# One Newton chain for the input norm's four tiles, mixer weights and last-tile statistics on VectorE, and the transposed memory reloaded in layer 1

## The chip, the cores and the metric

The kernel runs on one core of a Trainium2 chip. The metric is the device time of one execution in microseconds (us). Engines are named as in the profile: TensorE is PE (its weight loads PEld), VectorE is DVE, ScalarE is ACT, GpSimd is POOL, SyncE is SP, which here only issues transfers.

## The reference

A trunk of two layers over x (512 tokens, 1024 features), in float32, behind an input layer norm. Each layer has three parts, and each part ends in `h = layer_norm(alpha * h + part)`:

```
h = layer_norm(x, ln0_g, ln0_b)
for l in range(2):
    mix = hybrid_mixer(h, ...)            # u = silu(layer_norm(conv31(c_a * sigmoid(c_g)))),
                                          # o = rms_norm(gated linear attention(q, k, v, a)) * silu(r)
                                          # mix = concat([u, o]) @ w_mix_out
    h = layer_norm(alpha * h + mix, ln1)
    xa = memory_cross_attention(h, mem, w_xq, w_xkv, w_xo)   # K, V = split(mem @ w_xkv), 256 memory tokens, 4 heads
    h = layer_norm(alpha * h + xa, ln2)
    h = layer_norm(alpha * h + swiglu(h, w_ffn_in, w_ffn_out), ln3)
```

The mixer's causal depthwise convolution is 31 wide over 512 channels, its linear attention goes in chunks of 64 tokens with 4 heads.

## The kernel before, in words

The 512 tokens are four tiles of 128 (h[0] to h[3]). Every matrix product is done in three passes (`mm3`, L148 to L150): each operand is split into a high part, a rounded copy that ACT writes (L102), and a low part, the difference to it, that VectorE or POOL writes (L103); the products are high times high, low weight times high, and high weight times low. A weight chunk of 128x1024 is loaded by SP into one of four `raw` tiles (`wchunk`, L134), and its low part goes to the next engine of a list set by `wlo_engines` (L107).

Names in the rows: `mem` is the 256 memory tokens, `mT` its transpose (high and low, 1 MB each), made by TensorE's transposes into `mt` (`mem_T`, L621) and read by the key and value products of the cross-attention, `pp_xk` into `KT` and `pt_xv` into `V`. `w_c`, `w_qk`, `w_v`, `w_r` are chunks of the mixer's input weights, `w_xk`, `w_xv` of the memory's, `w_mo` of the mixer's output weights; `pp_c` is the convolution's input product. `cvt` and `cvb` are the transposes before and behind the convolution's own norm (`v_cln`, `y_cln`, `b`; `acc` is ACT's normalized result, L883), `csl` its silu, `cUh` and `cUl` the high and low parts of the result; `po`, `ms`, `y_rms`, `og`, `ogt`, `cOh` belong to the attention group's rms norm. `po_mo`, `po_xo`, `po_fo` are the three parts' output products.

The input norm (L665 to L677) works tile by tile: statistics (`bn_stats`, `bn_aggr`), then 1/sqrt by an integer guess and Newton steps (`rstd_of`, from L152: eleven VectorE instructions per tile with those around it), then b, then one ACT activation that scales h. `layer_norm` (L192) does the other norms: the sums of a tile come from the accumulating VectorE instruction that adds a product to h (L298), the squares from an ACT pass over the whole tile (L200), then two VectorE scalings by the mean (L206), the Newton steps, two scalings by the result (L211), and the transposes for the next product (`lt_ln`, L219, into `hT_ln`) or, behind the last norm, the store (L213).

In layer 1, `mem_T` loads the memory again (SP, L617) and transposes it again, among the mixer's input products. `aside` is a list of transfers that are issued one by one right behind weight loads (`behind`). A scheduler sets the order of the instructions on each engine from the order in the code, priorities and the buffers of its pools.

## Time and profile before

| | us |
|---|---|
| median of 3 runs | 1413.37 (1412.58, 1413.37, 1416.64) |
| profiled execution | 1412.22 |
| its span | 1410.5 |
| PE busy | 1379.3 (98%) |
| DVE busy | 1071.8 (76%) |
| ACT busy | 682.2 (48%) |
| POOL busy | 183.1 (13%) |

The span is the time between the first and the last instruction in the trace; the profiled execution's own time has 1.72 us around it. Busy time is the sum over an engine's instructions without those that only issue transfers. Times in timelines are counted from the start of the span.

### The profile page before, as it was taken

What the parts mean: (1) busy time and instruction counts of PE and PEld (TensorE: products, weight loads), DVE (VectorE), ACT (ScalarE), POOL (GpSimd) and SP (SyncE); (2) the same over time, 40 slices, a digit from 0 to 9 for tenths busy, and PEclk for the clock granted to TensorE, in tenths of its full rate; (3) what the DMA queues carried; (4) which work ended last, traced back from release to release, by engine and by line L of the source; (5) the groups of instructions that cost most, each with busy time, mean ns of one, the idle gap of its engine ahead of it and who ended that gap; (6) DMA issues with size and microseconds to landing.
All of it is one profiled execution on the core that took longest, in us unless ns stands there. A gap on an engine that the chain in (4) does not pass through costs nothing.

```text
span 1410.5 us, 22543 instructions
## 1 busy us (share of the span) xinstructions
PE 1379.3 (98%) x8847; PEld 1235.4 (88%) x8847; DVE 1071.8 (76%) x1911; ACT 682.2 (48%) x1122; POOL 183.1 (13%) x130
## 2 busy tenths in 40 slices
...
GB/s 256 154 90 91 90 168 146 256 237 134 76 153 147 220 164 138 180 181 126 101 141 89 90 91 164 239 151 257 204 61 123 176 141 197 171 135 203 156 135 60
DMA packets 131198, 214.80 MB, mean 152 GB/s; under 512 B 8956, under 2 KB 83408, under 8 KB 131092
## 3 DMA queue, kind: packets, MB, share of 16 engines
...
q10 hardware_dynamic: 288, 0.26, 0.1%
...
## 4 chain that ended last, share of the span: by engine, by line
PE 88%; DVE 4%; ACT 3%; DMA 3%; issue 1%; SPq 0%; DVEq 0%; ACTq 0%; POOLq 0%
PE fx L551 5%; PE fx L553 5%; PE fx L552 5%; PE fw L551 3%; PE fw L553 3%; PE fw L552 3%; PE pp_xq L149 2%; PE pp_xq L148 2%; PE pp_c L148 2%; PE pp_c L149 2%; PE pp_xq L150 2%; PE pp_c L150 2%; PE po_xo L148 2%; PE po_xo L149 2%; PE po_xo L150 2%; PE po_mo L148 2%
## 5 line engine op out<-in xcount | busy, mean ns | idle before, releaser
L750 DVE SCALAR_TENSOR_TENSOR cv<-u,chan,cv 128x511 f32<-128x511 f32 (+29 forms) x240 | 159.9, 729 | 0.2
L103 DVE TENSOR_TENSOR w_s<-s,w_s 128x1024 fp32r<-128x1024 f32 x80 | 97.7, 1221 | 38.3 <-ACT w_s L102 38.3
L102 ACT ACTIVATE w_s<-s 128x1024 fp32r<-128x1024 f32 x80 | 84.6, 1057 | 66.2 <-DMA s<-raw_a 42.1
L306 POOL DMA_DIRECT2D s<-raw_a x40 | 34.7, 880 | 628.6 <-DVE h L495 186.9
L551 PE MATMUL fx<-T_ln,w_s 128*128 128x256 f32 x320 | 90.7, 284 | 0.4 <-ACT u L564 0.2
L552 PE MATMUL fx<-T_ln,w_s 128*128 128x256 f32 x320 | 90.5, 283 | 0.0
L553 PE MATMUL fx<-T_ln,w_s 128*128 128x256 f32 x320 | 90.4, 283 | 0.0
L200 ACT ACTIVATE junk<-h,nm_ln 128x1024 uint8<-128x1024 f32 x24 | 27.6, 1150 | 113.2 <-DVE nm_ln L198 110.8
L102 ACT ACTIVATE w_a<-raw_a 128x1024 fp32r<-128x1024 f32 x60 | 63.1, 1057 | 30.6 <-PE foX_fo L514 13.0
L103 DVE TENSOR_TENSOR w_a<-raw_a,w_a 128x1024 fp32r<-128x1024 f32 x60 | 73.2, 1220 | 4.4 <-ACT w_a L102 4.1
L551 PEld LDWEIGHTS fx<-T_ln,w_s 128*128 128x128 f32 x320 | 61.4, 192 | 0.9 <-ACT u L564 0.8
L552 PEld LDWEIGHTS fx<-T_ln,w_s 128*128 128x128 f32 x320 | 61.4, 192 | 0.0
L553 PEld LDWEIGHTS fx<-T_ln,w_s 128*128 128x128 f32 x320 | 61.4, 192 | 0.0
L149 PE MATMUL pp_xq<-hT_ln,w_xq 128*128 128x256 f32 (+1 forms) x192 | 61.3, 322 | 0.0
L148 PE MATMUL pp_xq<-hT_ln,w_xq 128*128 128x256 f32 (+1 forms) x192 | 60.3, 321 | 0.5 <-ACT hT_ln L102 0.5
L150 PE MATMUL pp_xq<-hT_ln,w_xq 128*128 128x256 f32 (+1 forms) x192 | 60.1, 318 | 0.0
L149 PE MATMUL pp_c<-hT_ln,w_c 128*128 128x512 f32 (+1 forms) x160 | 56.6, 356 | 0.0
L148 PE MATMUL pp_c<-hT_ln,w_c 128*128 128x512 f32 (+1 forms) x160 | 55.4, 360 | 0.6 <-DVE h L298 0.4
L150 PE MATMUL pp_c<-hT_ln,w_c 128*128 128x512 f32 (+1 forms) x160 | 55.9, 351 | 0.0
L102 ACT ACTIVATE w_S_fo<-raw_S_fo 128x1024 fp32r<-128x1024 f32 x32 | 33.9, 1060 | 36.0 <-PE foX_fo L514 14.2
L149 PE MATMUL po_xo<-w_xo,oTh 128*128 128x512 f32 x128 | 49.9, 392 | 0.0
L306 POOL DMA_DIRECT2D S_fs<-w_ffn_out x16 | 17.2, 1073 | 249.1 <-DMA S_fs<-w_ffn_out 187.1
...
## 6 DMA issues: line engine op xcount, KB each, us to landing
raw_a<-w_ffn_in SPq DMA_DIRECT2D x60, 512.0 KB, 4.7
s<-raw_a POOLq DMA_DIRECT2D x40, 512.0 KB, 5.3
raw_fo<-w_ffn_out SPq DMA_DIRECT2D x36, 512.0 KB, 4.3
S_fs<-w_ffn_out SPq DMA_DIRECT2D x32, 512.0 KB, 5.3
raw_S_fo<-S_fs SPq DMA_DIRECT2D x32, 512.0 KB, 3.7
s<-w_ffn_in SPq DMA_DIRECT2D x20, 512.0 KB, 3.5
raw_xv<-w_xkv SPq DMA_DIRECT2D x16, 512.0 KB, 5.7
raw_c<-w_in SPq DMA_DIRECT2D x16, 512.0 KB, 5.0
```

Source lines behind the costliest of these rows:

```text
L102: ACT.activation(hi, src, AF.Copy)
L103: eng.tensor_sub(lo, src, f(hi))
L148: PE.matmul(o, lh, rh, start=start, stop=False)
L149: PE.matmul(o, lh, rl, start=False, stop=False)
L150: PE.matmul(o, ll, rh, start=False, stop=stop)
L200: ACT.activation(junk, ht, AF.Square, bias=nm, accum_out=v)
L306: POOL.dma_start(dst, src, accum_op=ALU.add, max_dma_last_dim=4096)
L551: PE.matmul(o, wh, bh, start=start and k == 0, stop=False, skip_group_check=True)
L552: PE.matmul(o, wh, bl, start=False, stop=False, skip_group_check=True)
L553: PE.matmul(o, wl, bh, start=False, stop=stop and k == 3, skip_group_check=True)
L750: DVE.scalar_tensor_tensor(cv[ct][:, s:], u[:, ct, :T - s], wj, cv[ct][:, s:], ALU.mult, ALU.add)
```

## The change

It has five parts.

1. The input norm collects the statistics of the four tiles in one table and runs one chain of Newton steps on 128x4 elements; all four ACT activations come behind it. In front of it, the low parts of the second half of `w_xv` are all made by VectorE, where VectorE and POOL took turns.
2. The low parts of layer 0's `w_mo` are all made by VectorE, where VectorE and POOL took turns (layer 1 had VectorE before).
3. In each of the six norms behind a product, the last token tile takes its mean and variance from VectorE's `bn_stats` and `bn_aggr`, without the accumulating sums and ACT's square. In the last norm of all the statistics go by 256 columns, in the others by 512.
4. Layer 0 writes the transposed memory, high and low, to DRAM (two SP transfers of 1 MB, behind the first two loads of `raw_xk`). Layer 1 reads them back with two transfers that POOL issues, and has no loads, transposes and splits of the memory.
5. Two tables that are used once move from a pool of their own to a shared one.

The diff, without the lines that only move a name:

```diff
@@ -81,7 +81,7 @@
     ident = const.tile([P, P], F32, name="ident")
     make_identity(nc, ident)
     causal = const.tile([P, CH], U8, name="causal")
-    causal_f = const.tile([P, CH], F32, name="causal_f")
+    causal_f = tmp.tile([P, T], F32, tag="t", name="causal_f")[:, :CH]
 
     POOL.memset(causal_f, 1.0)
     for i in range(2):
@@ -191,15 +191,19 @@
 
     def layer_norm(tt, sums, gb, name, hT=None, store=None):
 
+
         ht = h[tt]
         nm = small.tile([P, 1], F32, tag="nm", name=f"nm_{name}{tt}")
-        for x in sums[2:]:
-            DVE.tensor_scalar(sums[0], sums[0], x, None, ALU.add)
-        DVE.tensor_scalar(nm, sums[0], sums[1], -1.0 / D, ALU.add, ALU.mult)
         v = small.tile([P, 1], F32, tag="v", name=f"v_{name}{tt}")
-        ACT.activation(junk, ht, AF.Square,
-                       bias=nm, accum_out=v)
-        DVE.tensor_scalar(v, v, VS / D, VS * EPS, ALU.mult, ALU.add)
+        if isinstance(sums, list):
+            DVE.tensor_scalar(nm, sums[0], sums[1], -1.0 / D, ALU.add, ALU.mult)
+            ACT.activation(junk, ht, AF.Square, bias=nm, accum_out=v)
+            DVE.tensor_scalar(v, v, VS / D, VS * EPS, ALU.mult, ALU.add)
+        else:
+            mv = small.tile([P, 2], F32, tag="mv", name=f"mv_{name}{tt}")
+            DVE.bn_aggr(mv, sums)
+            DVE.tensor_scalar(v, mv[:, 1:2], EPS, VS, ALU.add, ALU.mult)
+            DVE.tensor_scalar(nm, mv[:, 0:1], -1.0, None, ALU.mult)
         tail = store is not None and tt == NT - 1
         for i in range(2):
             s = slice(i * 512, (i + 1) * 512)
@@ -293,12 +297,18 @@
                 cs = slice(*cols[c])
                 mm3(bks[c][:, :cols[c][1] - cols[c][0]], stat[k][0][:, tsl], stat[k][1][:, tsl],
                     wh[:, 0, cs], wl[:, 0, cs], k == 0, k == nk - 1)
-            st = small.tile([P, 3], F32, tag="sums", name=f"sums_{name}{tt}") if norm is not None else None
+            sw = 256 if last and fin else 512
+            if norm is not None:
+                st = ln_stats(tt, name, D // sw) if last else \
+                    small.tile([P, 2], F32, tag="sums", name=f"sums_{name}{tt}")
             for c, (c0, c1) in enumerate(cols):
-                DVE.scalar_tensor_tensor(h[tt][:, c0:c1], h[tt][:, c0:c1], scale, bks[c][:, :c1 - c0],
-                                         ALU.mult, ALU.add, accum_out=st[:, c:c + 1] if norm is not None else None)
+                DVE.scalar_tensor_tensor(h[tt][:, c0:c1], h[tt][:, c0:c1], scale, bks[c][:, :c1 - c0], ALU.mult, ALU.add,
+                                         accum_out=st[:, c:c + 1] if norm is not None and not last else None)
+                if norm is not None and last:
+                    for x0 in range(c0, c1, sw):
+                        DVE.bn_stats(st[:, x0 // sw, :], h[tt][:, x0:x0 + sw])
             if norm is not None:
-                norm(tt, [st[:, c:c + 1] for c in range(len(cols))])
+                norm(tt, st if last else [st[:, c:c + 1] for c in range(2)])
 
 
     def add_into(dst, src):
@@ -606,6 +616,18 @@
             dest.first(j, sg, uu)
 
 
+    mdram = [dram.tile([P, NK, MEM], F32, tag=f"mT{j}", name=f"mT{j}_dram") for j in range(2)]
+
+    def mem_views(mT):
+        return lambda kt: (mT[0][:, kt, :], mT[1][:, kt, :])
+
+    def mem_again(l):
+
+        mT = [block([P, NK, MEM], F32R, f"mT{j}_{l}") for j in range(2)]
+        for j in range(2):
+            POOL.dma_start(mT[j], mdram[j])
+        return mem_views(mT)
+
     def mem_T(name):
 
         mT = [block([P, NK, MEM], F32R, f"mT{j}_{name}") for j in range(2)]
@@ -622,7 +644,7 @@
                 ks, ms_ = slice(i * 4, i * 4 + 4), slice(mt * P, (mt + 1) * P)
                 split(mT[0][:, ks, ms_], mT[1][:, ks, ms_], pt.rearrange("p (k t) -> p k t", k=4))
 
-        return lambda kt: (mT[0][:, kt, :], mT[1][:, kt, :]), part
+        return mT, part
 
     def new_K(l):
         return [block([P, NK, MEM], F32R, f"KT{j}_{l}") for j in range(2)]
@@ -645,16 +667,16 @@
         for tt in tts:
             nc.sync.dma_start(h[tt], a["x"][0, tt * P:(tt + 1) * P, :])
 
-    mT, mem_part = mem_T("0")
+    mT_tiles, mem_part = mem_T("0")
+    mT = mem_views(mT_tiles)
     mem_part((0, 0))
-    lnrow = const.tile([2 * NK, P], F32, name="lnrow")
+    lnrow = tmp.tile([P, T], F32, tag="t", name="lnrow")[:2 * NK, :P]
     V = new_V(0)
     wlo_engines(DVE)
     mem_V(0, mT, V, 0, first=lambda: mem_part((1, 0), (0, 1), (1, 1)))
     load_x(0, 1, 2, 3)
     nc.sync.dma_start(lnrow[0:NK, :], a["ln0_g"].rearrange("(k p) -> k p", p=P))
     nc.sync.dma_start(lnrow[NK:2 * NK, :], a["ln0_b"].rearrange("(k p) -> k p", p=P))
-    wlo_engines(DVE, POOL)
     mem_V(0, mT, V, 1)
     pl = bank("lncol_ps", tag="tr")
     PE.transpose(pl[:, :2 * NK], lnrow, ident[:2 * NK, :2 * NK])
@@ -663,18 +685,19 @@
     KT = new_K(0)
     hT = new_hT("ln0")
     with tc.high_priority(offset=HP):
+        mv0 = const.tile([P, NT, 2], F32, name="mv0")
+        v0 = const.tile([P, NT], F32, name="v0")
+        b0 = const.tile([P, NT], F32, name="b0")
         for tt in range(NT):
             st = ln_stats(tt, "ln0")
             for i in range(2):
                 DVE.bn_stats(st[:, i, :], h[tt][:, i * 512:(i + 1) * 512])
-            mv = small.tile([P, 2], F32, tag="mv", name=f"mv_ln0{tt}")
-            DVE.bn_aggr(mv, st)
-            v0 = small.tile([P, 1], F32, tag="v", name=f"v_ln0{tt}")
-            DVE.tensor_scalar(v0, mv[:, 1:2], EPS, VS, ALU.add, ALU.mult)
-            y0 = rstd_of(v0, 1, f"ln0{tt}")
-            b0 = small.tile([P, 1], F32, tag="b0", name=f"b_ln0{tt}")
-            DVE.scalar_tensor_tensor(b0, mv[:, 0:1], -1.0, y0, ALU.mult, ALU.mult)
-            ACT.activation(h[tt], h[tt], AF.Identity, scale=y0, bias=b0)
+            DVE.bn_aggr(mv0[:, tt, :], st)
+        DVE.tensor_scalar(v0, mv0[:, :, 1], EPS, VS, ALU.add, ALU.mult)
+        y0 = rstd_of(v0, NT, "ln0")
+        DVE.scalar_tensor_tensor(b0, mv0[:, :, 0], -1.0, y0, ALU.mult, ALU.mult)
+        for tt in range(NT):
+            ACT.activation(h[tt], h[tt], AF.Identity, scale=y0[:, tt:tt + 1], bias=b0[:, tt:tt + 1])
         for k in range(NK):
             pt = bank(f"lt_ln0_{k}", tag="tr")
             for tt in range(NT):
@@ -802,8 +825,7 @@
             residual0(0, 1)
         wlo_engines(POOL)
         if l > 0:
-            mT, mem_part = mem_T(f"{l}")
-            mem_part((0, 0), (1, 0), (0, 1), (1, 1))
+            mT = mem_again(l)
             KT = new_K(l)
         conv_taps(0)
         gates()
@@ -963,6 +985,9 @@
         if l > 0:
             V = new_V(l)
             wlo_engines(DVE)
+        if l == 0:
+            for j in range(2):
+                aside.append(lambda j=j: nc.sync.dma_start(mdram[j], f(mT_tiles[j])))
         mem_K(l, mT, KT, 0)
         gla_pair(0)
         run(proj_r)
@@ -977,6 +1002,7 @@
             gla_pair(1)
 
 
+        wlo_engines(DVE)
         gb = load_gb(a["ln1_g"][l], a["ln1_b"][l], n_("ln1"))
         stat = [(cUh[:, i, :], cUl[:, i, :]) for i in range(4)] + [(cOh[:, i, :], cOl[:, i, :]) for i in range(4)]
         hT = new_hT(n_("ln1"))
```

The order of the instructions shows three places where more than the diff's lines move. Rows are line, operation, output and inputs, shape; the numbers behind names are buffers and differ between the two programs.

VectorE, layer 0, end of the convolution's norm, before:

```order
L162 TENSOR_TENSOR t_cln_0_1774<-y_cln_0_1773,v_0_1754 128x2
L163 TENSOR_TENSOR t_cln_0_1774<-t_cln_0_1774,y_cln_0_1773 128x2
L103 TENSOR_TENSOR KT_0_305<-pp_xk_001_1600,KT_0_304 128x256
L169 SCALAR_TENSOR_TENSOR s_cln_0_1775<-t_cln_0_1774 128x2
L169 SCALAR_TENSOR_TENSOR y_cln_0_1773<-s_cln_0_1775,y_cln_0_1773 128x2
L879 SCALAR_TENSOR_TENSOR b_0_1755<-mv_0_1753,y_cln_0_1773 128x2
L103 TENSOR_TENSOR w_mo_1932<-raw_mo_1930,w_mo_1932 128x1024
L103 TENSOR_TENSOR cUl_1244<-csl_0_1794,cUh_1243 128x512
L103 TENSOR_TENSOR cUl_1244<-csl_0_1803,cUh_1243 128x512
L103 TENSOR_TENSOR w_mo_1952<-raw_mo_1950,w_mo_1952 128x1024
L945 TENSOR_SCALAR ms_0_1873<-ms_0_1873 128x8
L103 TENSOR_TENSOR KT_0_305<-pp_xk_000_1663,KT_0_304 128x256
```

The same place in the changed program:

```order
L169 SCALAR_TENSOR_TENSOR y_cln_0_1737<-t_cln_0_1738,y_cln_0_1737 128x2
L103 TENSOR_TENSOR w_mo_1896<-raw_mo_1894,w_mo_1896 128x1024
L162 TENSOR_TENSOR t_cln_0_1738<-y_cln_0_1737,v_0_1718 128x2
L163 TENSOR_TENSOR t_cln_0_1738<-t_cln_0_1738,y_cln_0_1737 128x2
L169 SCALAR_TENSOR_TENSOR s_cln_0_1739<-t_cln_0_1738 128x2
L169 SCALAR_TENSOR_TENSOR y_cln_0_1737<-s_cln_0_1739,y_cln_0_1737 128x2
L901 SCALAR_TENSOR_TENSOR b_0_1719<-mv_0_1717,y_cln_0_1737 128x2
L103 TENSOR_TENSOR w_mo_1901<-raw_mo_1899,w_mo_1901 128x1024
L103 TENSOR_TENSOR cUl_1206<-csl_0_1758,cUh_1205 128x512
L103 TENSOR_TENSOR KT_0_307<-pp_xk_000_1627,KT_0_306 128x256
L103 TENSOR_TENSOR cUl_1206<-csl_0_1767,cUh_1205 128x512
L103 TENSOR_TENSOR KT_0_307<-pp_xk_001_1628,KT_0_306 128x256
```

A `w_mo` part stands inside the chain that ends in b (another stands some 13 rows ahead of this piece, before the `attT` copies), and the last `KT` parts stand ahead of `ms`, not behind it. On TensorE, ten more `pp_xk` matmuls stand ahead of the attention's `po` products at this place, so that fewer are left to stand between the `cvb` transposes.

VectorE, from layer 0 to layer 1: the last product's sum into h[3] (L298, now L305) and what follows it, before:

```order
L103 TENSOR_TENSOR w_c_110_7102<-raw_c_110_7100,w_c_110_7102 128x1024
L298 SCALAR_TENSOR_TENSOR h_105,sums_fo_03_7029<-h_105,po_fo_0_3_1_6992 128x512
L211 SCALAR_TENSOR_TENSOR h_104<-h_104,y_ln_02_6966,gb_ln_0_6735 128x512 x2
L103 TENSOR_TENSOR hT_ln_0_6740<-lt_ln_01_0_6903,hT_ln_0_6738 128x4x128
L103 TENSOR_TENSOR hT_ln_0_6741<-lt_ln_01_1_6911,hT_ln_0_6739 128x4x128
L198 TENSOR_SCALAR nm_ln_03_7032<-sums_fo_03_7029 128x1
L103 TENSOR_TENSOR w_c_111_7107<-raw_c_111_7105,w_c_111_7107 128x1024
```

and in the changed program:

```order
L171 TENSOR_SCALAR y_ln_02_6936<-s_ln_02_6938,y_ln_02_6936 128x1
L305 SCALAR_TENSOR_TENSOR h_105<-h_105,po_fo_0_3_1_6962 128x512
L103 TENSOR_TENSOR hT_ln_0_6710<-lt_ln_01_0_6873,hT_ln_0_6708 128x4x128
L103 TENSOR_TENSOR hT_ln_0_6711<-lt_ln_01_1_6881,hT_ln_0_6709 128x4x128
L215 SCALAR_TENSOR_TENSOR h_104<-h_104,y_ln_02_6936,gb_ln_0_6705 128x512 x2
L309 BN_STATS st_fo_03_6999<-h_105 128x6
L103 TENSOR_TENSOR w_c_111_7080<-raw_c_111_7078,w_c_111_7080 128x1024
```

The low parts of `hT_ln` come two scalings earlier. On TensorE the transposes of tile 2 (`lt_ln_02`), which stood right behind the first four `pp_c` matmuls, stand 24 matmuls later.

ACT, layer 1, end of the mixer, before:

```order
L102 ACTIVATE V_1_7974<-pt_xv_1_1_8540 128x512
L102 ACTIVATE w_mo_8818<-raw_mo_8816 128x1024
L891 ACTIVATE csl_1_8688<-cvb_1_8683,chan 128x512
L891 ACTIVATE csl_1_8697<-cvb_1_8692,chan 128x512
L102 ACTIVATE w_mo_8833<-raw_mo_8831 128x1024
L102 ACTIVATE cUh_7969<-csl_1_8688 128x512
L102 ACTIVATE cUh_7969<-csl_1_8697 128x512
L960 ACTIVATE cOh_7971<-ogt_1_8775,chan 128x4x128
```

and in the changed program:

```order
L102 ACTIVATE w_mo_8755<-raw_mo_8753 128x1024
L102 ACTIVATE V_1_7916<-pt_xv_1_0_8481 128x512
L913 ACTIVATE csl_1_8630<-cvb_1_8625,chan 128x512
L913 ACTIVATE csl_1_8639<-cvb_1_8634,chan 128x512
L102 ACTIVATE cUh_7911<-csl_1_8630 128x512
L102 ACTIVATE V_1_7916<-pt_xv_1_1_8482 128x512
L102 ACTIVATE w_mo_8760<-raw_mo_8758 128x1024
L102 ACTIVATE cUh_7911<-csl_1_8639 128x512
L102 ACTIVATE w_mo_8770<-raw_mo_8768 128x1024
```

The third `cUh` part stands ahead of any `w_mo` behind its `csl`, the fourth behind one.

## Rows read from the trace of the kernel before

**Rows 1.** The page: busy time and share of each engine, what all transfers moved in 40 slices of the span, and the engines' shares of the chain that ended last.

```profile
PE 1379.3 (98%) x8847; PEld 1235.4 (88%) x8847; DVE 1071.8 (76%) x1911; ACT 682.2 (48%) x1122; POOL 183.1 (13%) x130
...
GB/s 256 154 90 91 90 168 146 256 237 134 76 153 147 220 164 138 180 181 126 101 141 89 90 91 164 239 151 257 204 61 123 176 141 197 171 135 203 156 135 60
...
PE 88%; DVE 4%; ACT 3%; DMA 3%; issue 1%; SPq 0%; DVEq 0%; ACTq 0%; POOLq 0%
```

**Rows 2.** TensorE's timeline at the places of the change: start, duration, engine, line, operation, output and inputs, tile, and in brackets how long the engine was idle just before and what ended that.

```profile
38.81 1.78 PE L681 MATMUL lt_ln<-ident,h 128*128 128x128 f32 x8 [3.42 <-ACT xf L683]
...
192.68 0.55 PE L889 MATMUL cvb<-ident,acc 128*128 128x128 f32 x3 [0.87 <-ACT acc L883]
...
205.44 0.50 PE L148 MATMUL po_mo<-w_mo,cUh 128*128 128x512 f32 x1 [2.77 <-DVE KT L103]
...
708.97 0.62 PE L148 MATMUL pp_c<-hT_ln,w_c 128*128 128x256 f32 x3 [0.25 <-ACT hT_ln L102]
709.97 0.39 PE L148 MATMUL pp_c<-hT_ln,w_c 128*128 128x256 f32 x1 [0.39 <-DVE h L298]
711.90 1.12 PE L219 MATMUL lt_ln<-ident,h 128*128 128x128 f32 x4 [1.54 <-DVE hT_ln L103]
...
900.46 0.50 PE L148 MATMUL po_mo<-w_mo,cUh 128*128 128x512 f32 x1 [1.76 <-ACT cUh L102]
```

**Rows 3.** Stretches behind the four long gaps: its bounds and length, busy time (and instructions) of PE, PEld, DVE, ACT and POOL, TensorE's granted clock as a share of full speed, the transfers' share, and GB/s.

```profile
38.80:43.20 4.40, 4.39 (x16) 3.57 (x17) 3.38 (x5) 3.77 (x6) 0.00 (x0) 0.61 0.61 140
...
206.50:209.90 3.40, 3.40 (x10) 2.63 (x9) 3.38 (x4) 1.06 (x1) 2.22 (x1) 0.50 0.88 288
...
711.60:715.10 3.50, 3.20 (x15) 3.20 (x16) 3.31 (x8) 2.54 (x6) 0.00 (x0) 0.51 0.63 175
...
900.40:904.00 3.60, 3.54 (x15) 2.93 (x16) 3.60 (x6) 2.63 (x5) 0.00 (x0) 1.00 0.86 285
```

**Rows 4.** The start, timelines of POOL, VectorE and ACT.

```profile
23.83 5.75 POOL L103 TENSOR_TENSOR w_xv<-raw_xv,w_xv 128x1024 fp32r<-128x1024 f32 x2 [21.03 <-ACT w_xv L102]
...
25.68 1.65 DVE L103 TENSOR_TENSOR w_xv<-raw_xv,w_xv 128x1024 fp32r<-128x1024 f32 x1
...
29.64 4.66 ACT L677 ACTIVATE h<-h,b_ln,y_ln 128x1024 f32<-128x1024 f32 x4 [4.04 <-DVE b_ln L676]
```

**Rows 5.** The end of layer 0's mixer, timelines of POOL and VectorE; the last row is VectorE's at the same place of layer 1.

```profile
199.34 5.70 POOL L103 TENSOR_TENSOR w_mo<-raw_mo,w_mo 128x1024 fp32r<-128x1024 f32 x2 [10.66 <-ACT w_mo L102]
...
191.51 1.23 DVE L103 TENSOR_TENSOR w_mo<-raw_mo,w_mo 128x1024 fp32r<-128x1024 f32 x1
...
202.75 2.31 DVE L945 TENSOR_SCALAR ms<-ms 128x8 f32<-128x8 f32 x1
204.98 0.41 DVE L103 TENSOR_TENSOR KT<-pp_xk,KT 128x256 fp32r<-128x256 f32 x1
...
889.96 0.17 DVE L945 TENSOR_SCALAR ms<-ms 128x8 f32<-128x8 f32 x1
```

**Rows 6.** Layer 1, TensorE's timeline at the memory's transposes.

```profile
738.21 1.03 PE L621 MATMUL mt<-ident,mem 128*128 128x128 f32 x8
739.00 3.93 PE L770 MATMUL al<-hT_ln,wa 128*32 128x512 f32 x16
...
745.74 0.60 PE L621 MATMUL mt<-ident,mem 128*128 128x128 f32 x4
746.09 0.48 PE L149 MATMUL pp_c<-hT_ln,w_c 128*128 128x512 f32 x1
```

**Rows 7.** Layer 0's loads: SP's queue, ACT's timeline, and the page's table of transfers (issuer, number, KB each, median us from issue to landing).

```profile
111.80 23.05 SPq L134 DMA_DIRECT2D raw_r<-w_in  x4
...
133.62 1.06 ACT L102 ACTIVATE w_r<-raw_r 128x1024 fp32r<-128x1024 f32 x1 [1.66 <-PE pt_v L150]
...
raw_xv<-w_xkv SPq DMA_DIRECT2D x16, 512.0 KB, 5.7
```

**Rows 8.** POOL and TensorE in layer 1's input products (timelines), and the largest group of POOL's DMA issues: number, busy time, mean ns of one, and the idle time before them by what ended it.

```profile
734.35 4.76 POOL L103 TENSOR_TENSOR w_c<-raw_c,w_c 128x1024 fp32r<-128x1024 f32 x2 [0.99 <-ACT w_c L102]
...
742.76 0.40 PE L148 MATMUL pp_c<-hT_ln,w_c 128*128 128x512 f32 x1
743.00 0.39 PE L149 MATMUL pp_c<-hT_ln,w_c 128*128 128x512 f32 x1
...
L306 POOL DMA_DIRECT2D s<-raw_a x40 | 34.7, 880 | 628.6 <-DVE h L495 186.9 <-PE pp_f L150 145.4 <-DVE w_s L103 56.1
```

**Rows 9.** ACT's timeline at two places of layer 1: a table load among the input products, and the end of the mixer.

```profile
730.89 1.28 ACT L732 ACT_TABLE_LOAD   x1
...
898.83 1.06 ACT L102 ACTIVATE w_mo<-raw_mo 128x1024 fp32r<-128x1024 f32 x1 [1.08 <-DMA raw_mo<-w_mix_out]
```

**Rows 10.** From layer 0 to layer 1, VectorE's timeline.

```profile
709.23 0.68 DVE L298 SCALAR_TENSOR_TENSOR h<-h,po_fo 128x512 f32<-128x512 f32 x1
...
709.83 1.41 DVE L211 SCALAR_TENSOR_TENSOR h<-h,y_ln,gb_ln 128x512 f32<-128x512 f32 x2
```

**Rows 11.** A group of the whole kernel: line, engine, operation, output and inputs, shape, number, busy time, mean ns of one, idle time before them.

```profile
L669 DVE BATCH_NORM_STATS2 st_ln<-h 128x6 f32<-128x512 f32 x8 | 5.0, 667 | 0.0
```

**Rows 12.** The tail, VectorE's timeline.

```profile
1400.63 0.42 DVE L298 SCALAR_TENSOR_TENSOR h<-h,po_fo 128x256 f32<-128x256 f32 x1 [0.15 <-PE po_fo L150]
...
1404.51 0.27 DVE L165 TENSOR_SCALAR t_ln<-y_ln,v_ln 128x1 f32<-128x1 f32 x1
```

## The prediction

> **What bounds the kernel now.** I read the page's busy shares and its chain first: TensorE is busy 98% of the span and carries 88% of the chain, so what can be won is matrix work that goes away, and time in which TensorE waits or runs at half clock [rows 1]. So the second view is TensorE's timeline, for rows with an idle time in brackets: of 31 us idle in all (1410.5 less 1379.3), four places that the change touches hold 3.42, 2.77, 2.18 (0.25, 0.39 and 1.54) and 1.76 us, and one more 0.87 [rows 2]. The third is the table of stretches with the granted clock: behind three of the four, TensorE runs at about half (1.2 instead of 2.4 GHz) for some 3.4 us, at 1.76 it does not [rows 3]. Half the work of 3.40 us is lost there, so each fall costs 1.7 us. The last view is each of those places, engine by engine.
>
> My sum is made against the profiled execution, 1412.22 us (span 1410.5 and 1.72 around it). The median of the runs shown is 1.15 us above it; I add that at the end.
>
> **Start.** The four norms need b before ACT may scale h; ACT began at 29.64, 4.04 us after its last work, and took 4.66 for four [rows 4]. The change makes 11 small VectorE instructions of 44, but all four activations now wait for one b, and three weight subtractions that POOL partly did (2 in 5.75 us) stand on VectorE inside that chain, where one that ran beside POOL took 1.65 [rows 4]. Two more at about 1.2, less the stalls, for 33 small ones gone: b comes at about 29.4. ACT's order before the first xf is as it was, so the gap of 3.42 stays, with its half clock. I take **-0.2** (-0.6 to +0.3).
>
> **Layer 0's mixer boundary.** TensorE stood 2.77 us for the last KT copy: VectorE's ms, 128x8, took 2.31 us until POOL's two w_mo were done at 205.04 (199.34 and 5.70), where the same line took 0.17 in layer 1; KT came at 204.98 [rows 5]. With POOL out of w_mo this stall goes, and the order puts the KT parts ahead of ms. In return two subtractions of 1.23 [rows 5] enter VectorE ahead of and inside the conv norm's chain, which ended before the w_mo at 191.51: it ends some 2.3 later, and ACT's acc, the conv transposes (already 0.87 late) and the first cUh with it. TensorE's order has some 10 more key matmuls ahead of these transposes, so po_mo starts about 1.2 later; its first 24 matmuls then run without the KT wait, and what is late next is the third cUh, behind ACT's w_mo and csl, for about 2 us. If the clock stays up across that wait the stage ends 1.6 earlier, if it falls 0.1 later. Rows lie on both sides (1.76 kept it, 2.77 lost it), so I take the middle, **-0.7** (-2.0 to +2.0: all of the 2.77, less 0.8, or the whole 2.3 passed on).
>
> **Memory in layer 1.** 16 transposes go: 8 occupy 738.21 to 739.00, and 4 hold the stream from 745.74 to 746.09 [rows 6], the last 4 likewise: 0.79 + 2 x 0.35 = **-1.5** (-1.5 to 0). Their four ACT and VectorE copies are off the path. In return SP writes 2 MB after the first two raw_xk of layer 0, and POOL reads them back between two w_c. SP's next load, raw_r, was issued at 111.80 and its first use on ACT at 133.62 waited for no transfer; with 5.7 us for the slowest kind of 512 KB load [rows 7], 16 us are spare. At that rate (four times 5.7) the writes take 23 us one after the other, but the next raw_xk and raw_r may run beside them. POOL's w_c pair started at 734.35 and had 4.76 to run, while TensorE takes up this half at 742.76 and spends 24 matmuls on the part ready before [rows 8]: at the 0.23 between them that is until 748.2, so w_c's second part, ready at 736.73, has 11 us. Two issues at 0.88 [rows 8] cost nothing. I take **0** (0 to +2). An added ACT table load (the order has one more) takes 1.28 [rows 9] on an engine with 48% load: 0 (0 to +1.3).
>
> Here a rule of the Trainium skill speaks against the change. The rows show POOL's largest group of DMA issues at a mean of 0.88 each with VectorE 76% busy [rows 1, 8]. The Trainium skill's page "SBUF — State Buffer", section "Who interferes with whom", has it that a transfer issued by GpSimd can be starved of descriptors while VectorE holds the port pair they share. By the rows the term is 0; by the rule it would be the hold less 11 us. The rows give no sign of such holds.
>
> **Layer 0 to layer 1.** VectorE's sum at 709.23 was followed by two scalings (709.83, 1.41) and only then by the low parts of hT that TensorE's transposes waited 1.54 for [rows 2, 10]. Now the low parts stand right behind the sum, and TensorE has the second-half transposes 24 matmuls later. The added statistics (0.67 each [rows 11]) push the sum by about 0.35: gaps of 0.25, 0.74 and 0.2 instead of 2.18, so -1.0; and no gap there is long enough to resemble those that lost the clock, so -1.7 more. **-2.7** (-3.2 to 0).
>
> **Layer 1's mixer boundary.** cUh waited on ACT behind a w_mo whose transfer came at 898.8 [rows 9]. ACT now has the third cUh ahead of that. The 1.76 could go whole, but the fourth cUh still stands behind a w_mo, and that transfer sets the next matmuls' weights. **-0.7** (-1.8 to +1.5).
>
> **Other last-tile norms.** Six ACT squares give way to VectorE statistics (0.67 per 512 [rows 11]); in front of the attention and FFN projections TensorE has gaps below 0.5, so 0.
>
> **Tail.** The last sum began at 1400.63 and the Newton chain's t at 1404.51, over ACT's square and two scalings, which take 1.41 as between the layers [rows 10, 12]. New statistics of 256 columns (half of 0.67 and a bit, 0.4) ahead of it push the sum 0.45; then 0.4, aggregate, v, nm and y at 0.2 to 0.25 each (to about 1402.2), and 1.41: t at 1403.6. **-0.9** (-1.3 to +0.2).
>
> Sum: -0.2 -0.7 -1.5 +0 -2.7 -0.7 +0 -0.9 = **-6.7**: 1405.5 against the profiled execution, **1406.7** against the median.
>
> **Rivals.** (B) The waits move and the clock does not come back. Between layers only the gap shrinks (-1.0), layer 0's mixer wait goes over to cUh and falls again (+0.1 to +0.5), layer 1's turns to the weights (0): -0.2 +0.5 -1.5 -1.0 -0.9 = -3.1, **1410.3**. For it: TensorE lost the clock at a longest gap of only 1.54; against it: 1.76 alone did not cost it.
> (C) Slower: the 2 MB write holds up raw_r. With 16 us spare, the loss is the write's time less 16, against -6.7. At a quarter of the 256 GB/s that the page's busiest slice moved [rows 1], 2.1 MB take 33 us: +17 - 6.7, **1423.7**. It decides from 27 us on (78 GB/s). Against it: 5.7 us for 512 KB is already 92 GB/s.
> (D) The reload holds POOL, as the rule above has it: held 16 us between the two w_c, TensorE waits 5 and the time is **1411.7**. Against it: the 40 issues of that mean.
> That the change does not do what it says can be left out: its order shows all parts.
>
> **Chances.** Forecast 0.60, B 0.28, C and like lateness of weights 0.08, D 0.04. Measurement can tell about 0.3%, 4.2 us, from no change: faster (below 1409.1) is the forecast, 0.60; B and D are within, 0.32; C slower, 0.08. All gains at their far ends make -10.4, 1403.0 against the median and 1401.8 against the profiled execution; the lower end is 1402. Upward the range takes in B and D, to 1413.5.
>
> **What would show it.** Right: no TensorE transposes from memory in layer 1; TensorE gaps below 1 us near 710 and granted clock 1.00 behind them; VectorE's ms in layer 0 at 0.17 as it is in layer 1 [rows 5]; po_mo of layer 0 starting about 1.2 later and waiting for cUh, not KT; t about 1 us nearer the last sum. Wrong: a granted clock of 0.5 near 711; ACT or VectorE waiting for raw_r or raw_xk; the first conv transposes of layer 0 more than 3 us late; new gaps in front of w_c or w_xv of layer 1.

## The result, and the profile after

The changed kernel takes **1401.59 us** (median of 6 runs, 1399.98 to 1402.74) against 1413.17 of the kernel before (6 runs on the same chip, 1412.58 to 1416.64): a ratio of 0.9914, 95% interval 0.9901 to 0.9926, or -12.1 us (-14.0 to -10.5). The prediction said 1406.7 in a range of 1402.0 to 1413.5. The sign is as forecast, and the places that the forecast named moved as it said, all but the tail. The time lies 0.4 us below the range: the terms for the two mixers were too small by 1.25 and 1.9 us, and 2.9 us more stand in no term of the sum. Three executions at a granted clock of 0.63 to 0.83 (one each of the kernel before, e5 and e15, 1530 to 2004 us) are left out of every ratio below. The profiled execution took 1399.98 (span 1398.3), 12.24 less than that of before.

The page of the changed kernel, busy time of each engine and the engines' shares of the chain that ended last:

```profile
PE 1371.5 (98%) x8831; PEld 1231.1 (88%) x8831; DVE 1074.5 (77%) x1897; ACT 673.8 (48%) x1107; POOL 167.6 (12%) x126
...
PE 93%; DVE 3%; ACT 3%; DMA 1%; issue 1%; SPq 0%; DVEq 0%; ACTq 0%
```

Against [rows 1], TensorE's share of the chain went from 88% to 93%, and its busy time fell by 7.8 us. Of these 1.8 are matrix work that went away, and 2.6 lie in the two places where the clock no longer falls (1.2 in layer 0's mixer, 1.4 between the layers); 0.9 lie in layer 1's mixer, and 2.1 in the attentions and the feed-forward parts (FFNs). TensorE's timeline at the places of [rows 2] (the same columns):

```profile
38.37 0.44 PE L704 MATMUL lt_ln<-ident,h 128*128 128x128 f32 x2 [3.35 <-ACT xf L706]
...
194.30 0.44 PE L911 MATMUL cvb<-ident,acc 128*128 128x128 f32 x2 [0.48 <-ACT acc L905]
...
198.54 0.66 PE L911 MATMUL cvb<-ident,acc 128*128 128x128 f32 x4 [0.63 <-ACT csl L913]
...
207.20 0.50 PE L148 MATMUL po_mo<-w_mo,cUh 128*128 128x512 f32 x1 [1.47 <-ACT cUh L102]
...
706.58 0.61 PE L148 MATMUL pp_c<-hT_ln,w_c 128*128 128x256 f32 x3 [0.25 <-ACT hT_ln L102]
707.68 0.39 PE L148 MATMUL pp_c<-hT_ln,w_c 128*128 128x256 f32 x1 [0.49 <-DVE h L305]
708.28 0.39 PE L149 MATMUL pp_c<-hT_ln,w_c 128*128 128x256 f32 x1 [0.22 <-DVE hT_ln L103]
...
888.88 0.50 PE L148 MATMUL po_mo<-w_mo,cUh 128*128 128x512 f32 x1
```

The 3.42 at the start is still 3.35. The 2.77 for `KT` is gone, and `po_mo` waits 1.47 for `cUh` in its place. Between the layers 2.18 became 0.96 in three pieces. The 1.76 in layer 1's mixer no longer appears in brackets at all. The granted clock behind these places (columns as in [rows 3]):

```profile
38.30:41.80 3.50, 3.43 (x13) 2.84 (x14) 2.87 (x4) 3.24 (x6) 0.00 (x0) 0.55 0.60 141
...
207.20:211.00 3.80, 3.80 (x16) 3.11 (x17) 3.73 (x10) 1.53 (x2) 0.00 (x0) 1.00 0.92 301
...
708.30:712.00 3.70, 3.70 (x31) 3.70 (x32) 3.70 (x6) 1.54 (x4) 0.00 (x0) 1.00 0.43 119
```

Two of the three falls to 1.2 GHz are gone, those at 206 and 712 of before; the one at the start stays, as forecast. VectorE's and ACT's timelines show the causes:

```profile
29.01 0.16 DVE L698 SCALAR_TENSOR_TENSOR b<-mv,y_ln 128x4 f32<-128x4 f32 x1
...
205.65 0.17 DVE L967 TENSOR_SCALAR ms<-ms 128x8 f32<-128x8 f32 x1
...
1388.73 0.41 DVE L305 SCALAR_TENSOR_TENSOR h<-h,po_fo 128x256 f32<-128x256 f32 x1
...
1391.52 0.27 DVE L165 TENSOR_SCALAR t_ln<-y_ln,v_ln 128x1 f32<-128x1 f32 x1
...
1392.88 1.67 DVE L215 SCALAR_TENSOR_TENSOR h<-h,y_ln,gb_ln 128x256 f32<-128x256 f32 x4
```

```profile
29.21 4.64 ACT L700 ACTIVATE h<-h,b,y_ln 128x1024 f32<-128x1024 f32 x4 [3.79 <-DVE b L698]
...
884.48 2.01 ACT L102 ACTIVATE w_mo<-raw_mo 128x1024 fp32r<-128x1024 f32 x2 [2.01 <-DMA raw_mo<-w_mix_out]
```

`ms` takes 0.17 with POOL idle, where it took 2.31 beside POOL's two `w_mo` [rows 5]. ACT's scaling starts 0.43 earlier than in [rows 4]. At the end `t` starts 2.79 after the last sum, against 3.88 in [rows 12].

### The profile page after: what moved, and what is told of

It reads as the page before. It is cut to its first block, busy times and chain, and to the rows that moved or that the text cites. A ratio compares the mean times of both kernels' runs of the same rounds, so it can differ in the third digit from the quotient of the medians.

```text
span 1398.3 us, 22473 instructions
## 1 busy us (share of the span) xinstructions
PE 1371.5 (98%) x8831; PEld 1231.1 (88%) x8831; DVE 1074.5 (77%) x1897; ACT 673.8 (48%) x1107; POOL 167.6 (12%) x126
## 4 chain that ended last, share of the span: by engine, by line
PE 93%; DVE 3%; ACT 3%; DMA 1%; issue 1%; SPq 0%; DVEq 0%; ACTq 0%
PE fx L561 5%; PE fx L563 5%; PE fx L562 5%; PE fw L563 3%; PE fw L562 3%; PE fw L561 3%; PE pp_xq L149 2%; PE pp_xq L148 2%; PE pp_c L149 2%; PE pp_xq L150 2%; PE pp_c L148 2%; PE pp_c L150 2%; PE po_xo L150 2%; PE foX_fo L523 2%; PE po_xo L149 2%; PE foX_fo L522 2%
## 5 line engine op out<-in xcount | busy, mean ns | idle before, releaser
L200 ACT ACTIVATE junk<-h,nm_ln 128x1024 uint8<-128x1024 f32 x18 | 20.7, 1150 | 99.6 <-DVE nm_ln L199 97.2
```

## The experiments

I cut the program into stages that begin with the first matmul of a named product in TensorE's timeline. "Mixer" runs from the first `pt_r` to the first `pp_xq`; "attention" from there to the first `pp_f`; "FFNs" is the first `pp_f` to the first `po_fo`, the sum of both layers; "boundary" runs from the first `lt_ln` behind layer 0's last `po_fo` to the first `al` of layer 1 (half of the memory's transposes lie in it), "conv" from there to `pt_r` (the other half). "Tail" is from TensorE's last matmul to the end of the span.

| kernel | mixer 0 | attention 0 / 1 | boundary | conv 1 | mixer 1 | FFNs | tail |
|---|---|---|---|---|---|---|---|
| before | 107.71 | 119.51 / 119.49 | 31.32 | 78.39 | 124.56 | 598.4 | 9.90 |
| before, again (e9) | 107.64 | 119.51 / 119.48 | 31.43 | 78.41 | 124.47 | 601.9 | 9.90 |
| after | 105.73 | 119.13 / 119.13 | 27.92 | 77.39 | 122.01 | 596.2 | 10.09 |
| after, again (e10) | 105.68 | 119.11 / 119.11 | 27.93 | 77.39 | 121.61 | 596.8 | 10.19 |
| e1, mixer weights alone | 105.64 | 119.47 / 119.48 | 31.40 | 78.41 | 126.28 | 598.8 | 9.90 |
| e2, statistics alone | 107.67 | 119.15 / 119.12 | 29.28 | 78.45 | 124.62 | 599.3 | 9.31 |
| e3, reload alone | 107.63 | 119.47 / 119.50 | 30.55 | 77.38 | 121.78 | 598.7 | 9.97 |
| e4, input norm alone | 107.65 | 119.49 / 119.49 | 29.90 | 78.48 | 124.63 | 596.7 | 9.90 |
| e6, without statistics | 105.69 | 119.47 / 119.48 | 30.49 | 77.39 | 122.77 | 597.2 | 9.99 |
| e7, without reload | 105.72 | 119.12 / 119.11 | 28.70 | 78.48 | 124.53 | 597.9 | 9.32 |
| e12, without mixer weights | 107.68 | 119.12 / 119.13 | 28.48 | 77.39 | 121.59 | 597.4 | 9.40 |

All but the FFNs and mixer 1 repeat within some 0.1 us in kernels that hold the same parts of the change (the boundary of e4 and e11 apart, of which below). e2 and e12 have one wait more in the boundary than the changed kernel, 0.25 for ACT's `hT_ln`, which makes it 0.5 to 0.6 longer.

The attention's 0.37 is no gain. In every kernel with the new statistics TensorE's order moves four of the `lt_ln` transposes from the attention's end behind the first `pp_f`, into the FFN's stage. First the kernel before, then the changed one:

```profile
369.95 0.60 PE L219 MATMUL lt_ln<-ident,h 128*128 128x128 f32 x4
370.30 0.36 PE L148 MATMUL pp_f<-B_ln,w_g 128*128 128x256 f32 x1
```

```profile
367.38 0.28 PE L148 MATMUL pp_f<-B_ln,w_g 128*128 128x256 f32 x1
...
367.86 1.03 PE L223 MATMUL lt_ln<-ident,h 128*128 128x128 f32 x8
```

The four hold the stream for 0.35 us (369.95 to 370.30). Measured to the third group of `lt_ln`, in front of which both orders have the same matmuls, the two attentions together went from 263.17 to 263.01, and the rest of the FFNs from 574.2 to 571.4.

### The four parts, each alone

e1 is the kernel before with one line ahead of the mixer's output projection:

```diff
+        wlo_engines(DVE)
```

> The kernel before with one part of the change alone: layer 0's w_mo low parts all on VectorE. Theory A (each place is moved by its own part, and parts add up): the whole of the 2.1 us that layer 0's mixer gained in the changed kernel comes from here; about 1411.1, VectorE's ms at 0.17 instead of 2.31 us, TensorE's wait there about 1.5 us and for cUh, granted clock 1.00 behind it, and nothing moves in layer 1. Rival (the gain needs the earlier Newton chain or the other parts ahead of it): within 0.7 us of before, with the clock at 0.5 behind the wait.

Measured: ratio 0.9985 (0.9974 to 0.9996), -2.1 us. Mixer 0 has the whole -2.0 that the full change has there, so this part alone explains it. In the profiled execution, the slowest of e1's ten (1413.11, their median is 1410.63), mixer 1 was 1.7 slower, and TensorE's timeline says why (before it, the wait that took the place of `KT`):

```profile
208.50 0.50 PE L148 MATMUL po_mo<-w_mo,cUh 128*128 128x512 f32 x1 [1.47 <-ACT cUh L102]
...
900.56 0.80 PE L148 MATMUL po_mo<-w_mo,cUh 128*128 128x512 f32 x1 [1.94 <-ACT cUh L102]
```

```profile
206.00:209.40 3.40, 1.93 (x9) 1.30 (x8) 3.22 (x9) 3.11 (x8) 0.00 (x0) 1.00 0.88 295
900.50:904.00 3.50, 3.44 (x8) 2.78 (x9) 3.50 (x6) 2.62 (x5) 0.00 (x0) 0.51 0.91 305
```

The clock stayed at 2.4 GHz across 1.47 and fell to 1.2 behind 1.94.

e2 is the kernel before with the statistics hunks alone (`ln_stats` and `bn_stats` in the last tile's loop, two table tiles moved to make room):

```diff
+                st = ln_stats(tt, name, D // sw) if last else \
+                    small.tile([P, 2], F32, tag="sums", name=f"sums_{name}{tt}")
...
+                if norm is not None and last:
+                    for x0 in range(c0, c1, sw):
+                        DVE.bn_stats(st[:, x0 // sw, :], h[tt][:, x0:x0 + sw])
```

> The kernel before with one part alone (and two small tables moved, without which it does not fit the memory): the last tile's statistics from bn_stats. Theory A: layer 0 to layer 1 gains 2.6 us (a gap of 1.54 gone and the clock at 1.00 behind it), the tail about 0.6 up to the last scaling, the rest nothing: about 1410. Theory B (the 1.3 to 3 us that the changed kernel gained in layer 1's FFN come from ACT, which has one square less at the head of the FFN): 2 to 3 us more, about 1407.5, and they appear between 1090 and 1325 us of the span.

Measured: 0.9996 (0.9983 to 1.001), -0.6 us; the profile has -2.0 at the boundary (the full change has 0.6 more, beside the transposes) and -0.6 in the tail, and +0.1 in attentions and FFNs together. The interval reaches only to -2.4, so that the times show less than the stages. The boundary's waits are those of the full change:

```profile
709.34 0.62 PE L148 MATMUL pp_c<-hT_ln,w_c 128*128 128x256 f32 x3 [0.25 <-ACT hT_ln L102]
710.45 0.38 PE L148 MATMUL pp_c<-hT_ln,w_c 128*128 128x256 f32 x1 [0.49 <-DVE h L305]
```

e3 is the kernel before with the memory's write and reload:

```diff
+        mT = [block([P, NK, MEM], F32R, f"mT{j}_{l}") for j in range(2)]
+        for j in range(2):
+            POOL.dma_start(mT[j], mdram[j])
...
-            mT, mem_part = mem_T(f"{l}")
-            mem_part((0, 0), (1, 0), (0, 1), (1, 1))
+            mT = mem_again(l)
```

> The kernel before with one part alone: the transposed memory written by layer 0 and read back in layer 1. Theory A: 1.6 us for the 16 transposes and 2.6 at the end of layer 1's mixer, where ACT's order puts the third cUh ahead of the w_mo that waits for its transfer: about 1409, TensorE's gap of 1.76 there below 0.3. Theory C (the gain in layer 1's FFN hangs on when its loads are issued, which this part shifts): 2 to 3 us more, about 1406.5. Rival from the prediction (the write delays raw_r): a new wait of TensorE between 110 and 150 us.

Measured: 0.9954 (0.9937 to 0.997), -6.5 us, the largest of the four. The transposes give 0.8 in the boundary and 1.0 in the conv, and mixer 1 gives 2.8 that the prediction had not put down to this part. These stages make -4.6. The time, 1406.8, lies nearer to Theory C's 1406.5 than to A's 1409, but the FFNs took 598.7, no less than before, which speaks against C.

e4 is the kernel before with the input norm's chain for four tiles:

```diff
+        DVE.tensor_scalar(v0, mv0[:, :, 1], EPS, VS, ALU.add, ALU.mult)
+        y0 = rstd_of(v0, NT, "ln0")
+        DVE.scalar_tensor_tensor(b0, mv0[:, :, 0], -1.0, y0, ALU.mult, ALU.mult)
```

> The kernel before with one part alone (and two small tables moved): one Newton chain for four tiles, w_xv's low parts on VectorE. Theory A: 0.4 to 0.5 us at the start and nothing else, about 1412.7; the gap ahead of the second half's transposes stays 3.4 us with the clock at about half behind it. Rival (VectorE's own work now holds b back): 0 to 1 us slower.

Measured: 0.9979 (0.9966 to 0.9992), -3.0 us. The first `pt_r` came 0.8 earlier than in the first profile of before; the second profile of before had it 1.4 earlier without any change. The other gain stands at places that this edit doesn't touch: the FFNs took 1.7 less, and the wait between the layers was 1.54, as in before, and the clock did not fall behind it:

```profile
711.58 0.66 PE L219 MATMUL lt_ln<-ident,h 128*128 128x128 f32 x4 [1.54 <-DVE hT_ln L103]
```

```profile
708.00:711.00 3.00, 1.42 (x8) 0.77 (x6) 3.00 (x6) 1.95 (x3) 0.00 (x0) 1.00 0.80 201
710.30:713.70 3.40, 2.12 (x18) 2.12 (x19) 3.37 (x7) 2.15 (x4) 0.00 (x0) 1.00 0.43 97
```

That made the boundary 1.4 shorter with no edit there. The four parts measured alone add up to -12.2, the whole change -12.1. That they agree so well is partly luck: each part's interval is 3 to 5 us wide, and e4's -3.0 holds a fall of the clock that didn't come.

### One part left out

> The changed kernel with w_mo's low parts again half on POOL. If the parts add up (theory A), it loses the 2.0 us of layer 0's mixer and nothing else: about 1403.6, TensorE's wait of 2.77 us for KT and the clock at 0.5 behind it come back. Rival (the other parts had already moved that place): as the changed kernel, 1401.6.

Measured: 0.9929 (0.9911 to 0.9947), -10.0. No row of its profile is used; e12 repeats it.

> The changed kernel with ACT's square again in the last tiles. Theory A: the gap of 1.54 between the layers comes back, the clock falls behind it in most executions, and the last scaling starts 0.6 later: about 1404.5, layer 1's FFN (from its first pp_f to its first po_fo) as long as in the changed kernel within 1 us, 297.6 to 299. Theory B (the square at the head of the FFN slows it): 1407, and layer 1's FFN back at 300.

Measured: 0.9922 (0.9906 to 0.9938), -11.0. The 1.54 is back at the boundary, and the fall of the clock with it:

```profile
710.77 1.11 PE L219 MATMUL lt_ln<-ident,h 128*128 128x128 f32 x4 [1.54 <-DVE hT_ln L103]
```

```profile
710.40:713.80 3.40, 3.03 (x14) 3.04 (x15) 3.34 (x7) 1.75 (x4) 0.00 (x0) 0.51 0.57 166
```

With ACT's square back, layer 1's FFN took 297.4, as in the changed kernel: the FFNs' gain in the first comparison (Theory B) isn't the square's. The stages of this profile make e6 some 3 us longer than the changed kernel outside the start and the FFNs, the times 1.1, with some 2 us of interval on either side.

> The changed kernel with the memory loaded and transposed again in layer 1. Theory A: 1.6 us of transposes and 2.6 at the end of layer 1's mixer come back: about 1405.8, with TensorE's gap of 1.8 to 1.9 for cUh behind w_mo. Theory C (the FFN's gain hangs on this part's loads): about 1408, with layer 1's FFN at 300.

Measured: 0.9948 (0.9928 to 0.9967), -7.4: 4.7 less than the whole change, so the reload is worth the most of the three parts that were left out (the statistics, in e6, 1.1; the mixer weights, in e5, 2.1; the input norm was not left out). TensorE's wait for `cUh` is back, 1.77. Both FFNs (298.8 and 299.1) lie among those with the reload, so Theory C falls as well.

### The clock, by filling a wait

e8 puts 24 transposes, whose results nobody reads, into layer 0's wait for `KT` in the kernel before:

```diff
+                if name == "mo_0" and tt == 0 and (k, c) == (1, 1):
+                    pd = bank("dummy", tag="cv")
+                    for q in range(24):
+                        PE.transpose(pd[:, q % 4 * P:(q % 4 + 1) * P], f(stat[1][0][:, q % 4 * P:(q % 4 + 1) * P]), ident)
```

> The kernel before with 24 transposes of data that nothing reads, put on TensorE where it waits 2.77 us for KT in layer 0's mixer (0.11 us each, 2.6 us). They take no wait away. If the half clock behind that wait comes from TensorE's idle time, the granted clock stays 1.00 there and the kernel gains about 1.7 us (1411.2); if it comes from something else at that place (the loads, the other engines), the clock falls as before and the time is that of before, or up to 0.3 slower.

TensorE's timeline and the stretch behind it:

```profile
201.96 2.78 PE L299 MATMUL dummy<-ident,cUh 128*128 128x128 f32 x24
204.91 0.50 PE L148 MATMUL po_mo<-w_mo,cUh 128*128 128x512 f32 x1 [0.17 <-DVE KT L103]
```

```profile
206.00:209.40 3.40, 3.40 (x16) 2.78 (x16) 3.37 (x3) 1.06 (x1) 2.15 (x1) 1.00 0.89 315
```

The wait is as long as it was, but TensorE is busy in it, and the clock stays at 2.4 GHz where all seven profiles with a wait of 2.74 to 2.78 here lost it. So the fall follows TensorE's idleness, not the place. TensorE was 1.5 us ahead of the kernel before until a new wait of 0.41 for `cUl`; the stage gained 0.84 of the 1.7. By time the ratio is 0.9962 (0.9947 to 0.9977), -5.4, more than expected; the profile has 0.8 in this stage, 0.8 in mixer 1 and 1.7 in the FFNs, and I have no rows that tie the last two to the edit.

e11 does the same with the start of the changed kernel, 28 transposes in the wait of 3.35:

```diff
+            if k == 2:
+                pd = bank("dummy", tag="cv")
+                for q in range(28):
+                    PE.transpose(pd[:, q % 4 * P:(q % 4 + 1) * P], h[3][:, q % 8 * P:(q % 8 + 1) * P], ident)
```

> The changed kernel with 28 transposes that nothing reads put where TensorE waits 3.4 us at the start for ACT's xf (3.1 us of work). No wait is taken away. If idle time of TensorE is what costs the clock there, the granted clock stays 1.00 near 38 us and the kernel gains 1.7 us: 1399.9. If not, nothing or up to 0.3 slower.

```profile
34.33 3.22 PE L705 MATMUL dummy<-ident,h 128*128 128x128 f32 x28
37.85 1.32 PE L708 MATMUL lt_ln<-ident,h 128*128 128x128 f32 x8 [0.30 <-ACT xf L710]
...
889.33 0.50 PE L148 MATMUL po_mo<-w_mo,cUh 128*128 128x512 f32 x1 [1.47 <-ACT cUh L102]
```

The clock stays up (no stretch of this execution before the end is below 1.00), and the first `pt_r` comes 1.8 us earlier than in the changed kernel. But the time is that of the changed kernel, 1402.01, ratio 0.9905 (0.9888 to 0.9921). Part of the gain was given back in layer 1's mixer, where ACT's timeline has:

```profile
884.93 2.01 ACT L102 ACTIVATE w_mo<-raw_mo 128x1024 fp32r<-128x1024 f32 x2 [3.35 <-DMA raw_mo<-w_mix_out]
```

ACT waited 3.35 for the same transfer where it waited 2.01 in the changed kernel, and `cUh` behind it came 1.47 late: mixer 1 took 123.36, not 122.0. SP issued the transfer 0.9 us earlier than in the changed kernel, but it landed 6.4 us after its issue, not 5.1; why isn't shown. The boundary took 0.6 more, since the scheduler moved TensorE's order there too and brought one more wait of 0.25 for `hT_ln`, and the FFNs took 598.7. So the clock is shown here, and the 1.7 us by time are not.

### The same kernels again

> The kernel before, unchanged, profiled a second time. Theory J (part of the difference between the two first profiles is scatter): layer 0's and layer 1's FFN (first pp_f to first po_fo) differ by 1 to 2 us from the first profile's 298.05 and 300.34, the clock falls again behind the waits of 3.4 and 2.8 us and may or may not fall behind those of 1.5 and 1.8, every other stage agrees within 0.4. Rival (the first profile is typical and the FFN gain belongs to the change): both FFNs within 0.4 of the first profile.

> The changed kernel, unchanged, profiled a second time. Theory J: FFN lengths off by 1 to 2 us from the first profile's 298.6 and 297.6, layer 0's mixer, the layer boundary and layer 1's mixer within 0.3 of it, one fall of the clock (behind the start's wait) besides the end's. Rival: the FFNs within 0.4 of the first profile.

> The changed kernel with w_mo half on POOL, again, since the first profile of it is of no use: TensorE's wait of 2.77 us for KT and the clock at 0.5 behind it, layer 0's mixer 2.0 us longer than in the changed kernel, the other stages alike.

Measured: e9 0.9995 (0.998 to 1.0009), e10 0.9902 (0.9881 to 0.9924), e12 0.9926 (0.9899 to 0.9953). The table of stretches, FFN of layer 0 and of layer 1, first of before again, then of the changed kernel:

```profile
368.85:669.43 300.58, 298.97 (x2176) 283.44 (x2174) 239.87 (x358) 163.87 (x267) 18.35 (x21) 1.00 0.58 160
1062.56:1363.92 301.36, 299.60 (x2175) 283.60 (x2174) 239.72 (x358) 163.59 (x267) 17.38 (x20) 1.00 0.58 160
```

```profile
367.38:665.96 298.58, 298.19 (x2178) 283.90 (x2177) 241.22 (x359) 162.88 (x265) 18.36 (x21) 1.00 0.57 162
1051.74:1349.36 297.62, 297.37 (x2177) 283.70 (x2176) 241.90 (x359) 163.71 (x265) 17.38 (x20) 1.00 0.58 162
```

Both run at full clock. The same kernel before took 298.0 and 300.3 in its first profile, 300.6 and 301.4 in its second: 3.5 us of difference with no change of the program. The changed kernel's second profile differs by 0.1 and 0.7. TensorE's idle time, the stretch less its busy time, is 1.8 us in e9's layer 1 and 0.3 in the changed kernel's; in e9's it stands at a few places:

```profile
1182.72 0.47 PE L512 MATMUL foX_fo<-w_S_fo,pB_p 128*128 128x512 f32 x1 [0.44 <-DVE h L495]
1200.43 0.39 PE L551 MATMUL fx<-T_ln,w_s 128*128 128x256 f32 x1 [0.45 <-ACT u L564]
1303.12 0.47 PE L512 MATMUL foX_fo<-w_S_fo,pB_p 128*128 128x512 f32 x1 [0.47 <-DVE h L495]
```

So TensorE waited for VectorE's sums into `h` (L495) and for ACT's `u`. VectorE had waited 13 us in all for transfers of `raw_a` in that layer, 3.6 in the changed kernel's; that late transfers cause it is not shown.

### The tail

The tail was to become 0.9 shorter and became 0.2 longer. Transfers of the changed kernel's last 5.5 us (queues with packets, MB and share; issues with the median us to landing):

```profile
q14 instruction: 1, 0.01, 0.8%
...
out_dram<-h ACTq DMA_DIRECT2D x2, 128.0 KB, 2.4
```

A block of instructions is loaded among the last stores. Of the profiles up to e12 only those of e10 and e11 have one there too, and these three alone have a tail above 10. e13 and e14 shift VectorE's count of instructions, e15 ACT's; e13 by 24 and e14 by 8 memsets of one column at the start (e13 in the changed kernel, e14 in e12), e15 so:

```diff
-    DVE.memset(reset[:, 0::CH], 0.0)
+    DVE.memset(reset[:, 0::CH], 0.0); fil = const.tile([P, 1], F32, name="fil"); DVE.memset(fil, 0.0); [ACT.activation(fil, fil, AF.Copy) for _ in range(8)]
```

> The changed kernel with 24 more VectorE memsets of one column at its start, where that engine has idle time; every other engine's order is the same. The question is the tail: from VectorE's last scalings to the end 5.42 and 5.4 us in the two profiles of the changed kernel, 4.6 to 4.7 in all kernels whose last stores share the transfer engines with no instruction load. Theory K (an 8 KB block of VectorE's instructions is loaded among the last stores, because its count of instructions, 2295, ends just there): with 24 more the block is loaded well before, the table of transfers of the last 5 us has no instruction row, the stores land after 1.7 us, not 2.4, and from TensorE's end to the span's end it takes 9.3 to 9.4 us, not 10.1 to 10.2. Rival L (the stores land late because of the changed kernel's own order at its end): 10.1 and 2.4 us as before. By time 0.8 us can't be told; the FFN's six stretches give one more sample (Theory J, scatter: the sum of the two FFNs anywhere between 596 and 599).

> The changed kernel without VectorE's part of the mixer weights (as e12), with 8 more memsets of one column on VectorE: its count of instructions goes from 2287 to 2295, that of the changed kernel. Theory K: the instruction block lands among the last stores as in the changed kernel, the tail goes from 9.40 us to about 10.1. Rival L: it stays at 9.4.

> The changed kernel with 8 more activations of one column on ACT at its start (and one memset for them on VectorE), where both have idle time; the order on every engine is otherwise the same. Theory K, with ACT in VectorE's place: in the three profiles with a late tail (changed kernel, e10, e13) the last instruction load begins 3.0 to 3.2 us before the end, when ACT has run 1474 of its 1477 instructions (it has just issued its first output store), and ACT's second store follows 0.7 us after the first where others have 0.4 to 0.5; in all others with the new statistics it begins at 15.5 to 22.5 us before the end, at 1471 to 1472 of 1479 to 1484. It goes by ACT's count. With 8 more it begins about 16 us before the end, the last 5 us hold none, and from TensorE's end to the end it takes 9.3 to 9.4 us, not 10.1 to 10.2; 0.8 us can't be told from the times (1400.7 against 1401.5). Rival L (the changed kernel's order at its end): 10.1.

Measured: e13 0.9933 (0.9911 to 0.9955), tail 10.06, with the block among the stores; e14 (1403.50, one run) tail 9.40, without. So not VectorE's count. e15: 0.9937 (0.9919 to 0.9955), tail 9.41, and its last 5.5 us hold no `instruction` row:

```profile
q1 hardware_dynamic: 288, 0.26, 14.7%
q10 hardware_dynamic: 288, 0.26, 14.4%
...
out_dram<-h ACTq DMA_DIRECT2D x2, 128.0 KB, 1.7
```

With 8 more activations at the other end of the program the block is loaded 24.8 us before the end (I had said 16), the last stores land after 1.7 and not 2.4, and the tail is 0.7 shorter. Theory K holds with ACT's count: the four profiles with 1477 instructions on ACT (after, e10, e11, e13) have the block at the end, the one with 1485 has not. e15's time was no shorter than the changed kernel's (median 1403.65), since its FFNs took 299.8 and 300.5:

```profile
367.74:667.56 299.82, 299.07 (x2177) 283.99 (x2176) 241.30 (x359) 162.72 (x265) 18.38 (x21) 1.00 0.58 161
1053.13:1353.60 300.47, 298.86 (x2177) 283.89 (x2176) 241.16 (x359) 162.92 (x265) 17.41 (x20) 1.00 0.58 161
```

Its order from the first transposes on is that of the changed kernel, engine by engine: this is the scatter of Theory J on the side of the change too, 596.2 to 600.3.

## Why the prediction was right and where it was wrong

Two steps of the sum failed. In layer 1's mixer I bounded the gain by the wait of 1.76 and took less than half of it, on the ground that a transfer of `w_mo` would take the wait's place; -2.6 came. In layer 0's mixer I took the mean of two cases in place of one of them; -1.95 came, not -0.7. The tail went the other way than forecast, which took 1.1 back. Term by term:

**Start**: -0.2 forecast, about -0.35 measured (on the mean of nine profiles with this part the first `pt_r` comes 0.8 earlier than in the first profile of before, on that of six without it, that first one among them, 0.5; single profiles lie up to 1.2 from these, so that this is not told from nothing). `b` came at 29.01, forecast 29.4. The gap and its clock stayed, as said.

**Layer 0's mixer: the size.** -0.7 forecast, -1.95 measured. Each step came: POOL out of `w_mo`, `ms` at 0.17, `KT` no longer waited for, `cvb` later (gaps of 0.48, 0.63 and 0.27 where there was one of 0.87), `cUh` waited for behind ACT's `w_mo`. I had the wait at about 2 and took the middle between keeping and losing the clock; the wait was 1.47, and the clock was kept in all eight profiles that have it. A mean of two cases is the value of neither: -1.6, the case written down for a clock that stays up, would have been the estimate to take.

**Memory's transposes**: -1.5 forecast, -1.8 measured. The writes and the reload cost nothing that shows, and rival C (raw_r held up) falls: e3's mixer 0 starts no later than before's. Rival D went by a rule of the Trainium skill, page "SBUF — State Buffer", section "Who interferes with whom", that a transfer issued by GpSimd can be starved while VectorE holds the ports. The reload's two issues on POOL took 0.59 and 0.55, and no wait appears in front of `w_c` at that place. The hold that the Trainium skill tells of isn't seen here, with VectorE 77% busy.

```profile
728.50 1.13 POOL L628 DMA_DIRECT2D mT<-mT_dram  x2
```

**Between the layers**: -2.7 forecast, -2.6 measured (3.4 less 0.8 of transposes). e6 shows it from the other side.

**Layer 1's mixer: the size, and the part.** -0.7 forecast, -2.6 measured, beyond the far end of -1.8 that I gave. All of it comes with the reload (e3 has it alone, e7 and e1 don't). The 1.76 went whole. I had expected `w_mo`'s transfer to take its place, and whether it does goes by how long this transfer takes. In all nine profiles with the reload SP issues it 68.8 us after the first `pt_r`. Where it landed 4.4 to 5.1 us after its issue (seven profiles, the changed kernel's two among them), TensorE waited 0.12 at most; at 5.8 (e6) it waited 0.88 and at 6.4 (e11) 1.47. In e6:

```profile
893.47 0.50 PE L148 MATMUL po_mo<-w_mo,cUh 128*128 128x512 f32 x1 [0.88 <-ACT cUh L102]
```

The other 0.8 is time between TensorE's starts: 0.3 of it went with the wait (the 16 `ogt` transposes in front of it took 1.58 in place of 3.64, 1.76 of them the wait), and the rest is spread over products that the new order runs in fewer pieces, 35 for 39 (`pa` took 1.41 in two, 1.66 in three). That fewer pieces are the cause was not tested. I had bounded the gain by the wait alone.

**Other last-tile norms**: 0 forecast, -0.15 for both measured to the common mark. The term was right; the 0.37 per attention in the table are transposes that the FFN's stage took over.

**Tail: the sign.** -0.9 forecast, +0.2 measured. The chain became shorter, but by less than forecast: from TensorE's end to the last scalings 4.70 in place of 5.27, -0.57. The statistics pushed the last sum by 0.5, as I had it, and from the sum to `t` it took 2.79, where I had 2.5. The row of the kernel before (the changed kernel's is shown above):

```profile
1405.87 1.67 DVE L211 SCALAR_TENSOR_TENSOR h<-h,y_ln,gb_ln 128x256 f32<-128x256 f32 x4
```

The instruction block among the stores then cost 0.7. Without it (e2, e7, e12, e15) the tail is 9.3 to 9.4, -0.5 to -0.6.

**Sum**: -0.35 -1.95 -1.8 -2.6 -2.6 -0.15 +0.2 = **-9.25**, where I had -6.7. What is left of -12.1 are the FFNs, which no term touched: 574.2 to 571.4 from the common mark in the first two profiles. Over six profiles with the FFN's old order (before, e1, e3, e4, e8, e9) they took 572.5 to 577.8, mean 574.4; over five with the changed one (after, e10, e11, e13, e15) 571.4 to 575.5, mean 573.1. A difference of 1.3 in spreads of 5 and 4 shows nothing; that the change shortens the FFNs by up to some 3 us can't be excluded and stays open. By the sum alone the time would be 1403.9 (1413.17 less 9.25), inside the range: it left the range by the FFNs, for which the range left no room.

Rival B is half refuted: two of the clocks came back (where the waits became 1.47 and less), and the wait in layer 0 did pass on to `cUh` as it says.
